# The head of a fused hybrid layer: four column tiles in three chunks, 640 raw columns, rescaling on two engines

## The chip, the cores and the metric

The kernel runs on one core of a Trainium2 chip. A core has five engines that run side by side, each with its own queue of instructions: TensorE (PE in the profile; its weight loads are PEld), VectorE (DVE), ScalarE (ACT), GpSimd (POOL) and SyncE (SP, which here only issues DMAs). An engine works through its queue in order; a semaphore wait at the front of a queue holds all that stands behind it. The metric is the device time of one execution in microseconds; the time before is the median of three runs, 475.52 us (475.46 to 475.56).

## The reference

One decoder layer over 1024 prompt tokens and 64 sample tokens (8 sequences of 8), 1088 token columns in all, in float32:

- `h = rmsnorm(x) * g_norm`, then one projection `proj = h @ w_in` with 3200 output columns, cut into nine parts `Bg, Cg, v, zA, a, g, zB, q, zX`.
- Group A: `Bg * dwconv3(Cg * v) * silu(zA)`. Group B: `u = a * sigmoid(g)`, a causal convolution with 31 taps, a LayerNorm and a swish, times `silu(zB)`. Group X: attention of `q` into 256 memory tokens, whose keys and values come from `rmsnorm(mem)`, times `silu(zX)`.
- The three groups side by side, times `w_out`, plus `x`, and a last RMSNorm. The convolution states and the keys and values are outputs too.

What matters here is that the RMSNorm of a token is one factor, `1/sqrt(mean(x*x)+eps)`, and that a factor per token (a column in the kernel's layout) can be multiplied in before the projection or behind it.

## The kernel before, in words

**Layout.** Channels lie on the partitions and tokens on the columns. The 1024 input channels are 8 slices of 128 (`k` from 0 to 7). The 3200 projected columns are 25 column tiles of 128 (`order`, L260; the first four are a0, a1, a2 and g0, `NHEAD = 4`). A column tile's result for a range of tokens (a chunk) is a sum over the 8 slices in one PSUM bank.

**Precision.** Each float32 value is split into a rounded high part and a low part (`hh`, `hl` for the tokens, `wh`, `wl` for the weights), and a product is three passes: high with high, high tokens with low weights, low tokens with high weights (`pass_k`, L535). So a column tile takes 3 x 8 products per chunk. High parts are made by a cast or copy (for the first four tiles `hw_hi`, L283; on ACT, on GpSimd for the first), low parts by a subtraction on DVE (`hw_lo`, L289).

**Tokens into slices.** x arrives as 9 row tiles of 128 tokens (`xt`, the last with 64). PE transposes a row tile's slice into a PSUM bank (`x_tr`, L235; `sd` banks, four of them), ACT writes `hh` from it times `g_norm` (`x_ev_hi`, L247) and DVE writes `hl` (`x_ev_lo`, L251). Then the bank is free.

**Chunks.** The four head tiles go through the tokens in the chunks of `HEAD` (L33), 256, 256, 256 and 320 columns, all four tiles before the next chunk; the other 21 tiles (`REST`) in chunks of 384, 384 and 320. The `groups` (L166) are the row tiles of each head chunk; `Norm` (L177) takes a group's squares on ACT (`square`, L184), a root on ACT and a short chain on DVE.

**Raw columns.** For the first `RAW = 512` columns the head does not wait for the norm: `hh` and `hl` hold x without its token factor, and the results get the factor when they leave PSUM (`take`, L403), as a row of factors that is the same on all partitions (`rrow`). The row is made by writing a diagonal matrix per row tile (`r_bc`, L1027), transposing it on PE (`r_tr`) and copying it on ACT (`r_cp`, L1042). The other head chunks have their row tiles scaled first (`scale`, `scale_act`). Since the 21 later tiles need scaled slices, the raw columns are later scaled in place, for each k (`rescale`, L218): DVE adds `hh` and `hl` into `t`, multiplies by `rrow`, ACT copies the high part to `hh`, DVE subtracts for `hl`.

**Startup and order.** `startup()` (L995) loads row tiles 0 and 1 in halves (one over ACT's queue), the weights of the head by slice (`hw_load`) and then the rest of x over SP; it runs `WARM` products of the identity on PE ahead of the data. It stands under `tc.manual_schedule()`, so its instructions keep the written order on each engine. The order around the first two chunks is written out, product by product: all four tiles advance together, slice by slice (`p(k, j)`, L1055), with the weight casts, the evacuations, the squares and the factor row between them. Behind it the planner orders the instructions by priority (their order in the program) and by when it reckons them ready; small pieces of work wait in `steps`, one of which `side()` (L119) runs after every fourth product of a pass. There lie the transposes of the fourth chunk, the rescaling, the split of tile 4's weights, the norm of the memory tokens and the transposes of the parameters. The taps of the long convolution are queued on DVE at a lower priority (`run_taps`). SBUF tiles come from one pool of 45 (`big`).

Of the kernel before, what the change touches and what calls it, by code (L numbers as in the profile page):

```python
# [9 lines left out]
F32 = mybir.dt.float32  # L10
# [5 lines left out]
D = 1024  # L16
KT = 8
# [10 lines left out]
L0, L1, L2 = 1, 3, 2  # L28
T1, T2 = 2, 2
TAPPRI = 100  # L30
WARM = 9

HEAD = [(0, 256), (256, 256), (512, 256), (768, 320)]  # L33
REST = [(0, 384), (384, 384), (768, 320)]


NHEAD = 4
RAW = 512


@with_exitstack
def hybrid_trunk_kernel(
# [36 lines left out]
    def B(s, dt=F32, cols=NT):  # L79
        return big.tile([128, cols], dt, tag="b", name=nm(s))  # L80
# [20 lines left out]
    def tr(out, in_, n):  # L101
        T.transpose(out, in_, ident[:n, :n])  # L102
# [60 lines left out]
    xt = [None] * 9  # L163
    xrows = [128] * 8 + [64]
    xcols = [i * 128 for i in range(9)]
    groups = [[0, 1], [2, 3], [4, 5], [6, 7, 8]]  # L166

    def x_src(i):
        return x_prompt[0, i * 128:(i + 1) * 128, :] if i < 8 else x_sample.rearrange("b t d -> (b t) d")

    def x_load(i):
        xt[i] = xt[i] or B("x", cols=D)
        if xrows[i] < 128:
            G.memset(xt[i][xrows[i]:], 0.0)
        nc.sync.dma_start(xt[i][:xrows[i]], x_src(i))

    class Norm:  # L177
        def __init__(self, ts, rows):
# [34 lines left out]
    def x_half(i, h, q):
        if h == 0:
            xt[i] = B("x", cols=D)
        q.dma_start(xt[i][:, h * 512:h * 512 + 512], x_src(i)[:, h * 512:h * 512 + 512])

    def rescale(k):  # L218
        a, b = hh[k][:, :RAW], hl[k][:, :RAW]
        t = B("t", cols=RAW)  # L220
        V.tensor_tensor(t, a.bitcast(F32), b.bitcast(F32), ALU.add)
        V.tensor_tensor(t, t, rrow[0][:, RAW:], ALU.mult)
        S.copy(a, t)
        V.tensor_sub(b, t, a.bitcast(F32))
        dv(1900)

    def gm_T():
        ps = SD()
# [173 lines left out]

    def take(dst, ps, off, n):  # L403
        if rawc[0]:
            V.tensor_tensor(dst, ps[:, :n], rrow[0][:, RAW + off:RAW + off + n], ALU.mult)
            dv(n / 0.96 + 70)
        else:
            S.copy(dst, ps[:, :n])
# [126 lines left out]
    def pass_k(n, c, ps, p, k):  # L535
        off, N = chunks(n)[c]
        h = hl if p == 2 else hh
        mm(
            ps[:, :N], w_block(n, k, p == 1), h[k][:, off:off + N],
            p == 0 and k == 0, p == 2 and k == KT - 1, N / 2.4,  # L540
        )

    def pass_(n, c, ps, p):
# [451 lines left out]
    def startup():  # L995
        V.memset(epst, EPS)
        make_identity(nc, ident)
        x_half(0, 0, nc.sync)
        x_half(1, 0, nc.scalar)
        hw_load(0)  # L1000
        nc.scalar.dma_start(graw, g_norm[0].rearrange("(k p) -> k p", p=128))  # L1001
        hw_load(1, nc.scalar)
        S.activation(warm, epst, AF.Sqrt)
        hw_load(2)
        for i in (0, 1):
            x_half(i, 1, nc.sync)
        for k in (3, 4, 5):
            hw_load(k)
        x_load(2)
        for k in (6, 7):  # L1010
            hw_load(k)
        for i in range(3, 8):
            x_load(i)
        for k in range(KT):
            hh[k] = B("hh", F32R)
            hl[k] = B("hl", F32R)
        wps = MM()
        for _ in range(WARM):
            T.matmul(wps[:, :128], ident, ident, start=True, stop=True)
# [3 lines left out]
        n0, n1, n2, n3 = (Norm([xt[i] for i in g], [xrows[i] for i in g]) for g in groups)  # L1023

        rrow[0] = B("rrow", cols=2 * RAW)

        def r_bc(norm, off):  # L1027
            norm.chain()
            norm.factor()
            for i in (0, 1):  # L1030
                o = off + i * 128
                V.tensor_scalar(rrow[0][:, o:o + 128], ident, 0.0, norm.f[:, i:i + 1], ALU.mult, ALU.add)
            dv(500)

        def r_tr(off):
            ps = SD()
            for i in (0, 1):
                o = off + i * 128
                tr(ps[:, i * 128:i * 128 + 128], rrow[0][:, o:o + 128], 128)
            return ps  # L1040

        def r_cp(off, ps):  # L1042
            S.copy(rrow[0][:, RAW + off:RAW + off + 256], ps[:, :256])

        banks = [SD() for _ in range(4)]
# [13 lines left out]
        def hi(k):
            x_ev_hi(0, k, banks[k])  # L1060

        def lo(k):
            x_ev_lo(0, k, banks[k])

        hw_hi(0, G.tensor_copy)
        hi(0)
        hi(1)
        hw_hi(1, S.copy)
        lo(0)
        lo(1)  # L1070
        hw_lo(0)
        p(0, 0)
        hi(2)
        hi(3)
        hw_hi(2, S.copy)
        hw_lo(1)
        lo(2)
        p(1, 0)
        lo(3)
        p(0, 1)  # L1080
        p(0, 2)
        hw_lo(2)
        p(2, 0)
        x_load(8)
        mem_load()
        load_params()
        nc.sync.dma_start(graw, g_mem[0].rearrange("(k p) -> k p", p=128))
        w_load(NHEAD)
        n0.square(0)
        hw_hi(3, S.copy)  # L1090
        banks += [SD() for _ in range(4)]
        for i in (0, 1):
            for k in range(4, 8):
                x0_tr(k, i)
        p(1, 1)
        p(1, 2)
        for k in range(4, 8):
            hi(k)
        hw_lo(3)
        for k in range(4, 8):  # L1100
            lo(k)
        t1 = []
        for k in range(3, KT):
            if k > 3:
                hw_hi(k, S.copy)
                hw_lo(k)
            p(k, 0)
            p(k - 1, 1)
            p(k - 1, 2)
# [208 lines left out]
```

## Time and profile before

| | |
|---|---|
| median of three runs | 475.52 us |
| profiled execution | 475.39 us |
| its span in the trace | 473.4 us |
| PE busy | 463.8 us (98%) |
| DVE busy | 332.7 us (70%) |
| ACT busy | 228.4 us (48%) |
| GpSimd busy | 4.8 us (1%) |
| first product of the head | 7.14 us |
| first product of column tile 4 | 68.10 us |
| granted TensorE clock | 0.996 |

Times inside the trace count from the start of the span. A row of the timeline gives start, duration, engine, line, operation, the tile written and the tiles read, the shape and how many such instructions stand in a row; in square brackets is how long the engine had been idle and what ended that. DVE's operations all carry L59 and PE's products L95, the lines of the helpers that record them; the tile names tell them apart: `mm` is a projection's result, `sd` a bank for transposes, `junk` a square, `rrow` the factor row. A row of busy times by stretch gives the stretch, its length, then the busy time of PE, PEld, DVE, ACT and POOL with the number of instructions, the granted clock, the DMA share and the GB/s.

### The profile page before, as it was taken

The page shows a single profiled execution, that of the slowest core. Times are in us where ns is not written, and L with a number is a line of the kernel's source. Part 1 is how long each engine was busy: PE and PEld are TensorE (multiplying, and loading weights), DVE is VectorE, ACT ScalarE, POOL GpSimd, SP SyncE. Part 2 cuts the span into 40 slices and gives each one's busy share as a digit, 9 for nine tenths or more (in the row PEclk, how much of TensorE's full clock was granted, in tenths as well). Part 3 has the DMA queues.
Part 4 walks back from the last instruction along what each step waited for, and adds up shares of the span by engine and source line. Part 5 has one row for each costly group of instructions (what it writes and reads, how often), then busy time and mean ns, then how long its engine had stood idle before and what let it go on. Part 6 is the DMA issues. An engine that isn't in the chain of part 4 may idle for free.

```text
span 473.4 us, 7529 instructions
## 1 busy us (share of the span) xinstructions
PE 463.8 (98%) x2933; PEld 435.2 (92%) x2933; DVE 332.7 (70%) x592; ACT 228.4 (48%) x596; POOL 4.8 (1%) x21
## 2 busy tenths in 40 slices
PE   8999999999999999999999999999999999999994
PEld 7998999999999999999999999899999988888884
DVE  3758999999978999997479598833563537333334
ACT  5584668700223649457646455557863534211111
POOL 3000000000000000000000000000000000000000
PEclk9999999999999999999999999999999999999998
DMA  8920163100380400111020531022501553311111
GB/s 296 369 88 3 48 196 109 48 1 0 91 222 9 126 1 2 44 46 46 0 82 10 177 91 45 1 60 90 168 11 44 169 209 117 129 46 44 44 65 70
DMA packets 36447, 40.44 MB, mean 85 GB/s; under 512 B 1743, under 2 KB 30325, under 8 KB 36405
## 3 DMA queue, kind: packets, MB, share of 16 engines
q1 hardware_dynamic: 36109, 39.44, 26.2%
q8 instruction: 23, 0.38, 0.3%
q10 hardware_dynamic: 304, 0.53, 0.3%
q14 instruction: 11, 0.09, 0.1%
HBM read 34.81 MB, written 5.42 MB: 85 GB/s over the span
## 4 chain that ended last, share of the span: by engine, by line
PE 93%; ACT 3%; DMA 1%; DVE 1%; issue 0%; ACTq 0%; DVEq 0%
PE mm L95 81%; PE sd L95 7%; PE sd L102 5%; DMA wr<-in_w_in_dram 1%; ACT sd L881 1%; ACT junk L187 1%; PE sd L866 1%; ACT L146 0%; ACT wh L310 0%; DVE t L59 0%; ACT mh L512 0%; ACT sz L510 0%; ACT wh L287 0%; ACT lnx L868 0%; ACTq L1001 0%
## 5 line engine op out<-in xcount | busy, mean ns | idle before, releaser
L95 PE MATMUL mm<-hh,wh 128*128 128x384 f32 (+2 forms) x632 | 120.1, 325 | 1.4 <-ACT hh L249 1.1
L95 PE MATMUL mm<-hl,wh 128*128 128x384 f32 (+2 forms) x632 | 118.3, 323 | 0.0
L95 PE MATMUL mm<-hh,wl 128*128 128x384 f32 (+2 forms) x632 | 116.5, 322 | 0.0
L59 DVE SCALAR_TENSOR_TENSOR accB<-u,prm,accB 128x1024 f32<-128x1024 f32 x90 | 115.2, 1280 | 1.3
L95 PEld LDWEIGHTS mm<-hh,wh 128*128 128x128 f32 x632 | 102.1, 188 | 4.6 <-ACT hh L249 1.7
L95 PEld LDWEIGHTS mm<-hl,wh 128*128 128x128 f32 x632 | 101.5, 189 | 1.5 <-issue 1.3
L95 PEld LDWEIGHTS mm<-hh,wl 128*128 128x128 f32 x632 | 101.6, 188 | 0.7 <-issue 0.3
L95 PE MATMUL mm<-wol,mh 128*128 128x512 f32 (+1 forms) x136 | 51.2, 377 | 0.0
L95 PE MATMUL mm<-woh,ml 128*128 128x512 f32 (+1 forms) x136 | 51.2, 377 | 0.0
L95 PE MATMUL mm<-woh,mh 128*128 128x512 f32 (+1 forms) x136 | 51.2, 377 | 0.0
L59 DVE TENSOR_TENSOR xres<-mm,xres 128x512 f32<-128x512 f32 (+2 forms) x19 | 12.4, 662 | 37.9 <-PE mm L95 37.7
L944 ACT ACTIVATE sd<-xres 128x512 f32<-128x512 f32 (+1 forms) x16 | 9.6, 600 | 56.1 <-DVE xres L59 56.1
L59 DVE TENSOR_TENSOR wl<-wr,wh 128x512 fp32r<-128x512 f32 x50 | 33.3, 685 | 3.1 <-ACT wh L310 2.5
L95 PEld LDWEIGHTS mm<-woh,ml 128*128 128x128 f32 x136 | 25.6, 188 | 4.7
L95 PEld LDWEIGHTS mm<-woh,mh 128*128 128x128 f32 x136 | 25.6, 188 | 4.7
L95 PEld LDWEIGHTS mm<-wol,mh 128*128 128x128 f32 x136 | 25.6, 188 | 4.7
L712 ACT ACTIVATE P<-sd,nb 128x256 f32<-128x256 f32 x32 | 14.7, 472 | 22.9 <-DVE nb L59 17.9
L362 ACT ACTIVATE prod<-us,prm 128x64 f32<-128x64 f32 x93 | 24.8, 345 | 0.1
L310 ACT CAST wh<-wr 128x512 fp32r<-128x512 f32 x42 | 24.7, 625 | 0.0
L510 ACT ACTIVATE sz<-mm 128x384 f32<-128x384 f32 (+1 forms) x24 | 11.3, 471 | 20.4 <-PE mm L95 20.3
L433 ACT ACTIVATE sig<-mm 128x384 f32<-128x384 f32 (+1 forms) x6 | 2.8, 473 | 37.4 <-PE mm L95 37.3
L249 ACT ACTIVATE hh<-sd,gT 128x256 fp32r<-128x256 f32 (+1 forms) x32 | 14.0, 490 | 8.8 <-PE sd L102 8.7
(195 smaller groups left out, 530.1 us busy)
## 6 DMA issues: line engine op xcount, KB each, us to landing
wr<-in_w_in_dram SPq DMA_DIRECT2D x21, 512.0 KB
wor<-in_w_out_dram SPq DMA_DIRECT2D x8, 512.0 KB
xres<-in_x_prompt_dram SPq DMA_DIRECT2D x8, 512.0 KB
out_dram<-xres SPq DMA_DIRECT2D x7, 512.0 KB
x<-in_x_prompt_dram SPq DMA_DIRECT2D x6, 512.0 KB
cache<-in_cache_mem_k_dram SPq DMA_DIRECT2D x8, 256.0 KB
cache<-in_cache_mem_v_dram SPq DMA_DIRECT2D x8, 256.0 KB
wr<-in_w_in_dram SPq DMA_DIRECT2D x7, 256.0 KB
```

The source lines that it names most:

```text
L59: r = f(*a, **k)
L95: T.matmul(out, lhsT, rhs, start=start, stop=stop)
L102: T.transpose(out, in_, ident[:n, :n])
L187: S.activation(junk[:r], self.ts[i][:r], AF.Square, accum_out=self.ss[:r, i:i + 1])
L249: S.activation(hh[k][:, off:off + n], ps[:, :n], AF.Copy, scale=gT[:, k:k + 1])
L310: S.copy(dst_hi[:, a:b], src[:, a:b])
L362: S.activation(p3[:, k, :], src, AF.Copy, scale=w[:, k0 + k:k0 + k + 1])
L510: S.activation(sz[0][:, off:off + n], ps[:, :n], AF.Silu)
L712: S.activation(P_[i][:, h * 256:h * 256 + 256], bank[h // 2][:, (h % 2) * 256:(h % 2) * 256 + 256], AF.Exp, bias=nb[:, h:h + 1], scale=SCA ...
L866: T.transpose(ps[:, j * 128:j * 128 + 128], accB[j][:, lncols[i]:lncols[i] + 128], ident)
L881: S.activation(junk[:, :384], t, AF.Square, bias=lst["nmu"][:, i:i + 1], accum_out=lst["sq"][:, i:i + 1])
L944: S.activation(junk[:rows], xr[:rows, cs], AF.Square, accum_out=ss[:rows, f:f + 1])
```

## The change

The head goes through three chunks of 256, 384 and 448 columns instead of four. The raw columns are the first two chunks, 640 instead of 512, and the norm groups are row tiles 0 and 1; 2 to 4; 5 to 8. Row tiles 0 and 1 are loaded whole, tile 1 over ACT's queue; the weights of slice 1 move from ACT's queue to SP's, and the order of the loads on SP is new. There is one warm-up product less. The first chunk is one loop over the slices, and in each slice the order of passes is high-high, low tokens, low weights. The sum of `hh` and `hl` in the rescaling moves to GpSimd (`rescale_sum`), with a tile of its own per slice, queued one slice ahead of the rest, which stays on DVE and ACT. The factor row gets its transposes and its copy in one function, behind slice 6 for the first chunk.

```diff
-WARM = 9
-HEAD = [(0, 256), (256, 256), (512, 256), (768, 320)]
+WARM = 8
+HEAD = [(0, 256), (256, 384), (640, 448)]
-RAW = 512
+RAW = 640
...
-    groups = [[0, 1], [2, 3], [4, 5], [6, 7, 8]]
+    groups = [[0, 1], [2, 3, 4], [5, 6, 7, 8]]
...
+    rs = {}
+
+    def rescale_sum(k):
+        rs[k] = B("t", cols=RAW)
+        G.tensor_tensor(rs[k], hh[k][:, :RAW].bitcast(F32), hl[k][:, :RAW].bitcast(F32), ALU.add)
 
     def rescale(k):
-        a, b = hh[k][:, :RAW], hl[k][:, :RAW]
-        t = B("t", cols=RAW)
-        V.tensor_tensor(t, a.bitcast(F32), b.bitcast(F32), ALU.add)
-        V.tensor_tensor(t, t, rrow[0][:, RAW:], ALU.mult)
+        a, b, t = hh[k][:, :RAW], hl[k][:, :RAW], rs[k]
+        V.tensor_tensor(t, t, rrow[0], ALU.mult)
         S.copy(a, t)
         V.tensor_sub(b, t, a.bitcast(F32))
...
     def startup():
...
-        x_half(0, 0, nc.sync)
-        x_half(1, 0, nc.scalar)
+        x_load(0)
+        x_load(1, nc.scalar)
         hw_load(0)
         nc.scalar.dma_start(graw, g_norm[0].rearrange("(k p) -> k p", p=128))
-        hw_load(1, nc.scalar)
         S.activation(warm, epst, AF.Sqrt)
-        hw_load(2)
-        for i in (0, 1):
-            x_half(i, 1, nc.sync)
-        for k in (3, 4, 5):
+        for k in range(1, 5):
             hw_load(k)
         x_load(2)
-        for k in (6, 7):
+        for k in (5, 6):
             hw_load(k)
-        for i in range(3, 8):
+        x_load(3)
+        hw_load(7)
+        for i in range(4, 8):
             x_load(i)
...
+        def r_tr(c):
+            off, n = HEAD[c]
             ps = SD()
+            for o in range(0, n, 128):
+                tr(ps[:, o:o + 128], fb[:, off + o:off + o + 128], 128)
+            S.copy(rrow[0][:, off:off + n], ps[:, :n])
...
+        for k in range(KT):
+            if k == 0:
+                hw_hi(0, G.tensor_copy)
+                hi(0)
+                hi(1)
+            else:
+                hw_hi(k, S.copy)
+            if k < 4:
+                if k > 1:
+                    hi(k)
+                lo(k)
+            hw_lo(k)
             for n in range(NHEAD):
-                pass_k(n, 0, acc[n], j, k)
...
+                pass_k(n, 0, acc[n], 0, k)
+            if k < KT - 1:
+                for j in (2, 1):
+                    for n in range(NHEAD):
+                        pass_k(n, 0, acc[n], j, k)
+            if k in (1, 2):
+                for m in (2 * k + 2, 2 * k + 3):
+                    t0.append(SD())
+                    x0_tr(m, 0)
+                    x0_tr(m, 1)
+            if k in (2, 3):
+                for m in (2 * k, 2 * k + 1):
+                    hi(m)
+                    lo(m)
+            if k == 1:
+                x_load(8)
+                mem_load()
+                load_params()
+                nc.sync.dma_start(graw, g_mem[0].rearrange("(k p) -> k p", p=128))
+                w_load(NHEAD)
+            if k in (3, 4):
+                n0.square(k - 3)
             if k == 5:
-                n0.square(1)
                 r_bc(n0, 0)
             if k == 6:
-                rps = r_tr(0)
+                r_tr(0)
+                n1.square(0)
                 t1 += [x_tr(1, 0), x_tr(1, 1)]
-        r_cp(0, rps)
-        x_ev_hi(1, 0, t1[0])
-        x_ev_hi(1, 1, t1[1])
+        n1.square(1)
+        for k in (0, 1):
+            x_ev_hi(1, k, t1[k])
         for n in range(NHEAD):
-            for j in (1, 2):
-                pass_k(n, 0, acc[n], j, KT - 1)
+            for j in (2, 1):
+                pass_k(n, 0, acc[n], j, KT - 1, 1)
             evac(n, 0, acc[n])
...
-        n1.square(0)
-        n1.square(1)
-        r_bc(n1, 256)
-        n2.square(0)
-        n2.square(1)
+        n1.square(2)
+        r_bc(n1, HEAD[1][0])
+        for i in range(4):
+            n2.square(i)
         n2.chain()
         n2.factor()
         n2.scale_act(0)
         n2.scale(1)
+        n2.scale(3)
+        n2.scale_act(2)
         for n in range(NHEAD):
             pass_(n, 1, acc[n], 1)
-        rps = r_tr(256)
-        r_cp(256, rps)
-        steps.extend([None, None])
+        r_tr(1)
         for k in range(KT):
             steps.append(mk(x_T, 2, k))
-        for i in range(3):
-            n3.square(i)
         for n in range(NHEAD):
             pass_(n, 1, acc[n], 2)
             evac(n, 1, acc[n])
         flush_steps()
-        n3.chain()
-        n3.scale(0)
-        n3.scale(1)
-        n3.scale(2)
...
             startup()
+        w_load(NHEAD + 1)
+        rescale_sum(0)
+        steps.append(mk(params_T, 0))
         for k in range(KT):
-            steps.append(mk(x_T, 3, k))
-        for k in range(KT):
-            steps += [mk(rescale, k), None]
-        for n in range(NHEAD):
-            proj(n, 2)
-        w_load(NHEAD + 1)
+            steps += [mk(rescale_sum, k + 1) if k < 7 else None, mk(rescale, k)]
         for h in range(2):
             steps.append(mk(w_split, NHEAD, h))
         steps.append(mem_norm)
-        for j in range(3):
-            steps += [mk(params_T, j), None]
+        for j in (1, 2):
+            steps.append(mk(params_T, j))
         steps.append(gm_T)
         for n in (0, 3, 1, 2):
-            proj(n, 3)
+            proj(n, 2)
         flush_steps()
```

More of the change, by code (lines that the diff above doesn't have):

```diff
@@ L165, in hybrid_trunk_kernel, with x_load @@
     xcols = [i * 128 for i in range(9)]
-    groups = [[0, 1], [2, 3], [4, 5], [6, 7, 8]]
+    groups = [[0, 1], [2, 3, 4], [5, 6, 7, 8]]
     def x_src(i):
         return x_prompt[0, i * 128:(i + 1) * 128, :] if i < 8 else x_sample.rearrange("b t d -> (b t) d")
-    def x_load(i):
+    def x_load(i, q=nc.sync):
         xt[i] = xt[i] or B("x", cols=D)
@@ L174, in x_load @@
             G.memset(xt[i][xrows[i]:], 0.0)
-        nc.sync.dma_start(xt[i][:xrows[i]], x_src(i))
+        q.dma_start(xt[i][:xrows[i]], x_src(i))
     class Norm:
@@ L211, in scale @@
                 dv(660)
[L213 to L216, printed above, removed]
+    rs = {}
+    def rescale_sum(k):
+        rs[k] = B("t", cols=RAW)
+        G.tensor_tensor(rs[k], hh[k][:, :RAW].bitcast(F32), hl[k][:, :RAW].bitcast(F32), ALU.add)
     def rescale(k):
-        a, b = hh[k][:, :RAW], hl[k][:, :RAW]
-        t = B("t", cols=RAW)
-        V.tensor_tensor(t, a.bitcast(F32), b.bitcast(F32), ALU.add)
-        V.tensor_tensor(t, t, rrow[0][:, RAW:], ALU.mult)
+        a, b, t = hh[k][:, :RAW], hl[k][:, :RAW], rs[k]
+        V.tensor_tensor(t, t, rrow[0], ALU.mult)
         S.copy(a, t)
         V.tensor_sub(b, t, a.bitcast(F32))
-        dv(1900)
+        dv(1500)
     def gm_T():
@@ L404, in take @@
         if rawc[0]:
-            V.tensor_tensor(dst, ps[:, :n], rrow[0][:, RAW + off:RAW + off + n], ALU.mult)
+            V.tensor_tensor(dst, ps[:, :n], rrow[0][:, off:off + n], ALU.mult)
             dv(n / 0.96 + 70)
@@ L533, in evac, with pass_k @@
             {"g": ev_g, "a": ev_a, "q": ev_q, "cg": ev_cg, "v": ev_v, "bg": ev_bg}[kind](c, ps, j)
-    def pass_k(n, c, ps, p, k):
+    def pass_k(n, c, ps, p, k, last=2):
         off, N = chunks(n)[c]
@@ L539, in pass_k @@
             ps[:, :N], w_block(n, k, p == 1), h[k][:, off:off + N],
-            p == 0 and k == 0, p == 2 and k == KT - 1, N / 2.4,
+            p == 0 and k == 0, p == last and k == KT - 1, N / 2.4,
         )
@@ L1022, in startup @@
         xt[8] = B("x", cols=D)
-        n0, n1, n2, n3 = (Norm([xt[i] for i in g], [xrows[i] for i in g]) for g in groups)
-        rrow[0] = B("rrow", cols=2 * RAW)
+        n0, n1, n2 = (Norm([xt[i] for i in g], [xrows[i] for i in g]) for g in groups)
+        rrow[0] = B("rrow", cols=RAW)
+        fb = B("fb", cols=RAW)
         def r_bc(norm, off):
@@ L1029, in r_bc, with hi, lo @@
             norm.factor()
-            for i in (0, 1):
+            for i in range(norm.n):
                 o = off + i * 128
-                V.tensor_scalar(rrow[0][:, o:o + 128], ident, 0.0, norm.f[:, i:i + 1], ALU.mult, ALU.add)
-            dv(500)
-        def r_tr(off):
+                V.tensor_scalar(fb[:, o:o + 128], ident, 0.0, norm.f[:, i:i + 1], ALU.mult, ALU.add)
+        def r_tr(c):
+            off, n = HEAD[c]
             ps = SD()
[L1037 to L1045, printed above, removed]
-        def x0_tr(k, i):
-            tr(banks[k][:, i * 128:i * 128 + 128], xt[i][:, k * 128:(k + 1) * 128], 128)
+            for o in range(0, n, 128):
+                tr(ps[:, o:o + 128], fb[:, off + o:off + o + 128], 128)
+            S.copy(rrow[0][:, off:off + n], ps[:, :n])
+        t0 = [SD() for _ in range(4)]
+        def x0_tr(k, i):
+            tr(t0[k][:, i * 128:i * 128 + 128], xt[i][:, k * 128:(k + 1) * 128], 128)
+        def hi(k):
+            x_ev_hi(0, k, t0[k])
+        def lo(k):
+            x_ev_lo(0, k, t0[k])
         for i in (0, 1):
@@ L1053, in startup @@
         acc = [MM() for _ in range(NHEAD)]
-        def p(k, j):
-            for n in range(NHEAD):
-                pass_k(n, 0, acc[n], j, k)
[L1059 to L1109, printed above, removed]
+        t1 = []
+        for k in range(KT):
[10 more added lines that the diff above has]
+            hw_lo(k)
+            for n in range(NHEAD):
+                pass_k(n, 0, acc[n], 0, k)
[20 more added lines that the diff above has]
+                n0.square(k - 3)
```

## The prediction

> **What bounds the kernel now.** I read the page first, then the busy time in two stretches, the head (first product to the first product of tile 4, 7.14 to 68.10 us) and the rest.
>
> ```profile
> span 473.4 us, 7529 instructions
> ...
> PE 463.8 (98%) x2933; PEld 435.2 (92%) x2933; DVE 332.7 (70%) x592; ACT 228.4 (48%) x596; POOL 4.8 (1%) x21
> ```
> ```profile
> 7.14:68.10 60.96, 59.59 (x463) 57.63 (x463) 50.22 (x129) 41.40 (x89) 2.70 (x9) 1.00 0.45 154
> 68.10:473.40 405.30, 398.79 (x2446) 372.60 (x2444) 282.13 (x462) 184.89 (x504) 0.20 (x2) 1.00 0.23 72
> ```
>
> PE sets the time, and everything that the change touches lies before 68.10. So the question is when tile 4 starts. The profiled execution took 475.39 us, 1.99 more than its span and 0.13 under the median of the runs; my sum goes against 475.39, and I add the 0.13 at the end.
>
> PE's busy figure hides short waits, so I take its pace from the starts of unbroken rows of its timeline:
>
> ```profile
> 10.23 1.03 PE L102 MATMUL sd<-ident,x 128*128 128x128 f32 x8
> ...
> 26.63 4.01 PE L95 MATMUL mm<-hh,wl 128*128 128x256 f32 x32
> ...
> 348.53 1.58 PE L95 MATMUL mm<-hh,wh 128*128 128x384 f32 x8
> ...
> 356.88 1.33 PE L95 MATMUL mm<-hh,wh 128*128 128x320 f32 x8
> ...
> 360.39 1.58 PE L95 MATMUL mm<-hh,wh 128*128 128x384 f32 x8
> ...
> 419.65 0.39 PE L95 MATMUL mm<-woh,mh 128*128 128x512 f32 x1
> ...
> 425.55 0.39 PE L95 MATMUL mm<-wol,mh 128*128 128x512 f32 x1
> ```
>
> A transpose costs (1.03-0.27)/7 = 0.109, where 0.27 is one transpose's own duration; a product of 256 columns (4.01-0.28)/31 = 0.1203; of 384, 48 in 8.35 us, 0.1740; of 320, 24 in 3.51 us, 0.1463; of 512, 26 in 5.90 us, 0.2269. Columns alone would make these proportional; they are not, each product has some 0.013 us of its own.
>
> The head holds 96 products a chunk (4 tiles, 8 k, 3 passes): 96 x (3 x 0.1203 + 0.1463) = 48.69; 77 transposes behind 7.14, 8.39; the small g_mem one 0.16. That is 57.24 of 60.96: **PE waits 3.72 us in the head.** The largest pieces:
>
> ```profile
> 7.14 0.71 PE L95 MATMUL mm<-hh,wh 128*128 128x256 f32 x4 [0.33 <-ACT hh L249]
> 8.21 0.74 PE L95 MATMUL mm<-hh,wh 128*128 128x256 f32 x4 [0.36 <-ACT wh L287]
> ...
> 34.70 0.71 PE L95 MATMUL mm<-hl,wh 128*128 128x256 f32 x4
> 36.17 1.11 PE L95 MATMUL mm<-hh,wh 128*128 128x256 f32 x3 [0.76 <-ACT hh L249]
> ```
>
> Four products need 0.48, so the second row is 0.6 late (a weight cast) and the fourth 1.0 (ACT was squaring the last row tiles).
>
> **The change part by part.**
>
> *Fewer products.* 448 columns lie midway between 384 and 512: 0.2005. 96 x (0.1203 + 0.1740 + 0.2005) = 47.50, **-1.19** (bounds of the 448 price, 0.1740 to 0.2269, give -3.7 to +1.3; the straight line is taken). One more transpose of a factor, **+0.11**.
>
> *The start.* Row tiles 0 and 1 come whole, so 1.31 MB (x0, x1, first weights) must land before the first product, where 0.79 MB did.
>
> ```profile
> 0.00:6.03 6.03, 4.65 (x22) 4.41 (x23) 0.23 (x2) 1.49 (x2) 0.83 (x10) 1.00 0.64 199
> ```
> ```profile
> 1.38 4.21 PE L1019 MATMUL mm<-ident 128*128 128x128 f32 x18 [1.38 <-POOL ss L182]
> ...
> 5.72 1.09 PE L102 MATMUL sd<-ident,x 128*128 128x128 f32 x8
> ...
> 6.03 0.61 POOL L287 CAST wh<-wr 128x512 fp32r<-128x512 f32 x1 [4.66 <-DMA wr<-in_w_in_dram]
> ...
> 6.52 0.84 ACT L249 ACTIVATE hh<-sd,gT 128x256 fp32r<-128x256 f32 x2 [2.86 <-PE sd L102]
> ...
> 7.03 0.88 DVE L59 SCALAR_TENSOR_TENSOR hl<-sd,gT,hh 128x256 fp32r<-128x256 f32 x2 [1.04 <-ACT hh L249]
> ```
>
> When the first weights were there (6.03, GpSimd's cast) 199 GB/s x 6.03 = 1.20 MB had moved: a third of it already belonged to later loads. In the new order nothing but x0, x1 and those weights is ahead, so 1.31 MB are there 0.11 MB, some 0.3 to 0.4 us, later. x0 and x1 lie on two queues (SP and ACT) and land before the weights; from there the steps are the old ones (cast 0.61, product). First product near 7.5: **+0.36**. Bounds: 0, and the whole 0.52 MB at 199 GB/s, +2.6; the value near 0 is taken because the moved bytes are counted, the other end assumes that no byte of the 1.20 MB was spare. The weights of k=7 now stand behind four row tiles: 4.2 MB, even at 199 GB/s 21 us, and ACT comes to them at 22 (below), so the rest of SP's new order costs nothing; ACT's queue issues one DMA fewer. x8, memory and parameters are issued about as early as before, for work behind 47 us.
>
> *The order on ACT.* Startup is ordered by hand, and the trace shows ACT keeping to it:
>
> ```profile
> 9.30 1.07 ACT L187 ACTIVATE junk<-x 128x1024 f32<-128x1024 f32 x1
> ...
> 10.35 0.61 ACT L287 CAST wh<-wr 128x512 fp32r<-128x512 f32 x1
> ...
> 12.41 1.16 ACT L287 CAST wh<-wr 128x512 fp32r<-128x512 f32 x2
> ...
> 13.45 1.08 ACT L187 ACTIVATE junk<-x 128x1024 f32<-128x1024 f32 x1
> ...
> 14.65 0.30 ACT L146 ACTIVATE y<-ss,epst 128x2 f32<-128x2 f32 x1
> ...
> 16.37 1.29 DVE L59 TENSOR_TENSOR wl<-wr,wh 128x512 fp32r<-128x512 f32 x2
> ...
> 17.82 0.38 PE L102 MATMUL sd<-ident,rrow 128*128 128x128 f32 x2
> ...
> 18.24 0.37 ACT L1043 COPY rrow<-sd 128x256 f32<-128x256 f32 x1 [2.26 <-PE sd L102]
> 18.51 0.84 ACT L249 ACTIVATE hh<-sd,gT 128x256 fp32r<-128x256 f32 x2
> ...
> 21.29 0.84 ACT L249 ACTIVATE hh<-sd,gT 128x256 fp32r<-128x256 f32 x2 [1.94 <-PE sd L102]
> ...
> 25.28 1.05 ACT L187 ACTIVATE junk<-x 128x1024 f32<-128x1024 f32 x1
> ...
> 29.90 0.29 ACT L146 ACTIVATE y<-ss,epst 128x2 f32<-128x2 f32 x1
> ...
> 31.22 1.15 ACT L205 ACTIVATE x<-x,f 128x1024 f32<-128x1024 f32 x1 [1.02 <-DVE f L59]
> 32.27 0.35 ACT L1043 COPY rrow<-sd 128x256 f32<-128x256 f32 x1
> ```
> ```profile
> L59 DVE SCALAR_TENSOR_TENSOR hl<-sd,gT,hh 128x256 fp32r<-128x256 f32 x24 | 10.5, 477 | 3.0 <-ACT hh L249 2.9
> ```
>
> ACT sat idle for 2.26 and 1.94 us, yet row tile 2 was squared only at 25.28: within startup nothing overtakes. From these rows, start to start: a cast holds ACT 0.51 (1.16 less one of 0.65), a square 1.04 (9.30 to 10.35), an hh evacuation 0.37 (0.84 less 0.47), a factor copy 0.27 (18.24 to 18.51), a row-tile scaling 1.05 (31.22 to 32.27). Handovers: last transpose to ACT 0.31 (17.93 to 18.24), cast to its product 0.67 (7.54, where the cast began, to 8.21), hh evacuation to hl 0.51 (6.52 to 7.03), square to root 1.20 (13.45 to 14.65), root to row-tile scaling 1.32 (29.90 to 31.22), root through the factor chain to the next weight subtraction 1.72 (14.65 to 16.37).
>
> In the old order the casts ran ahead of PE. The new order puts evacuations, squares and the factor copy between the casts, some of them behind PE's own work. Per k PE has 12 products, 1.44 us; 4 of them 0.48. PE then waits:
>
> - k=3: the transposes of slice 7 need slice 3's bank, whose evacuation stands behind those of slices 4 and 5 and a cast. Counted from the last transpose of slice 5: 0.09+0.37+0.37+0.51+0.51+0.48 (its hl) = 2.33, less PE's 0.11+1.44+0.22: **0.56**.
> - k=4: evacuation 7, a square, the cast, from the last transpose: 0.31+0.37+1.04+0.67 = 2.39, less 0.11+1.44: **0.84**. k=5: the second square lies between the casts, 0.51+1.04 less 1.44: **0.11**.
> - k=6: the low weights stand behind the factor chain on DVE. From k=5's cast: 0.64+0.60 (its subtraction), 1.59 (1.72, the root being done), 0.73 = 3.56, less 0.67+1.44+0.96: **0.49**.
> - k=7: the factor copy waits for PE's k=6, then a square, then the cast: 0.11+0.31+0.27+1.04+0.67 = 2.40, less 8 transposes (0.87): **1.53**; its low half another **0.10**.
> - chunk 1: a bank late, **0.10**. Then ACT does, behind its last evacuation, a square, a root, four squares, a root, two row-tile scalings: 0.31+0.47+1.20+0.20+4.32+1.32+1.05+1.20 = 10.07 from PE's last transpose to row tile 7; PE has 9.71 (0.11, 16 products 2.78, 32 products 5.57, 0.33, 0.70, 0.22): **0.36**. This takes the place of the 1.0 at 36.17.
>
> Together 4.09 against 3.72: **+0.37**. Ends: -2.7 if ACT is not held behind PE at k=4, 6 and 7 (1.4 left of the 4.09), +2.0 if one more square (1.04) and four slower handovers come in.
>
> *The rescaling.* Per k DVE loses one operation of three; the two left grow to 640 columns.
>
> ```profile
> L59 DVE TENSOR_TENSOR t<-t,rrow 128x512 f32<-128x512 f32 x8 | 5.4, 685 | 0.0
> ...
> L59 DVE TENSOR_TENSOR u<-mm,rrow 128x256 f32<-128x256 f32 x6 | 2.3, 417 | 3.5 <-PE mm L95 2.8 <-ACT rrow L1043 0.8
> ...
> masks.py:199 POOL TENSOR_SCALAR_AFFINE_SELECT ident<-ident 128x128 f32<-128x128 f32 x1 | 0.3, 292 | 0.0
> ```
> ```profile
> 60.97 0.69 DVE L59 TENSOR_TENSOR hl<-t,hh 128x512 fp32r<-128x512 f32 x1
> ```
>
> 512 columns hold DVE 0.60 (two in 1.29); the slope is (685-417)/256 = 1.05 ns a column, so 640 hold it 0.735: 16 x 0.735 = 11.8 against 24 x 0.60 = 14.4. The old rescaling ended at 61.66, 6.4 ahead of tile 4; it was hidden under PE's chunks, so the 2.6 that DVE gains are worth **0**, as are the fewer evacuations and the dropped third group of factors. GpSimd's addition is not in the trace: between its cast's 1.2 ns a column (0.76 for 640) and the select's 2.3 (1.46). I take 1.46, as the select too does more than copy: 8 are 11.7 us, beside 20 us of chunk-2 products, cost 0. If that cover is gone, DVE's products with the factor row are late, and tile 4's first pass behind them. The Trainium skill (GPSIMD Engine Reference, 3.1 Elementwise — side-by-side cycle accounting) gives some 2.6 cycles an element at 1.2 GHz for such an add, an estimate of 1.39; the sum would stay.
>
> Sum: -1.19+0.11+0.36+0.37 = **-0.35**: 475.0 against the profile's 475.39, 475.2 as a median. Tile 4 would begin at 67.75, chunk 1 end near 47.4. 0.2% (0.95 us) is about what a measurement of this kernel can tell from no change.
>
> **The rivals.**
>
> 1. *ACT is not held up* (faster). If the casts run ahead of PE after all, the -2.7 replaces the +0.37: 475.2-3.1 = 472.1; half of it 473.6. For it: ACT is busy 41.4 of 60.96 us, there is room. Against: the 2.26 us idle in front of a ready square.
>
> 2. *GpSimd's sums hold up the rescaling* (slower). If all sums come behind 47.4 and DVE's operations cannot run beside them, each k costs 1.46+1.47: 23.4 us, to 70.8. Tile 4's pass needs the last hh at 67.75+7 x 0.174 = 69.0, 1.8 before it is there; each of the taps that DVE takes in between adds its length, over 1 us. 477 to 480, say 478. It decides from a sum of 1.25 us on (8 x (1.25+1.47) = 21.7, what there is up to 69.0). Against: GpSimd is busy for 2.7 of the head's 60.96 us, and the sums could start once chunk 1's slices are evacuated, long before 47.4. The Trainium skill (SBUF — State Buffer, Who interferes with whom) has this as a rule: a VectorE operation with two SBUF inputs and a GpSimd operation that reads SBUF take one port pair as an exclusive lock. No trace of before shows the two side by side.
>
> 3. *PE is still slow when x arrives.* The 18 warm-up instructions took (4.21-0.42)/17 = 0.22 each, the transposes of the same shape 0.109: PE ran at half pace until some time before 5.9. With 16 of them and then a pause until x lands, it may stay there. Price: half of the time until it wakes, at most the same 4.3 us, so 0 to 2.1; about 1.2, since part of it is waiting anyway: 476.4. The Trainium skill (TensorE: Matmul & The Clock Gate, What's actually happening) says that the clock opens after a busy window of about 3.4 us that runs freely; 16 warm-ups fill 3.5, with nothing to spare.
>
> 4. *The new order costs more*: the +2.0 in place of +0.37, 476.8.
>
> **How the numbers follow.** The forecast with its own spread, 474.2 to 476.1 (starts from 7.1 to 8.2, waits 0.5 either way): 0.47, of which 0.04 is faster by over 0.2% and 0.03 slower. Rival 1: 0.28, all faster. Rival 2: 0.10 and rival 4: 0.05, all slower. Rival 3: 0.10, of which 0.04 within. Faster 0.32, within 0.44, slower 0.24. The range leaves out the far quarter of rival 1 and rival 2: 472.9 to 477.1.
>
> **What would show it.** First product near 7.5, tile 4 near 67.8. PE 1.5 us idle ahead of its k=7 products, ended by ACT's weight cast, and 0.8 ahead of k=4. No wait over 0.5 near 36 to 40. GpSimd's sums at 0.8 to 1.5 us, the last hl subtraction before 66, no wait of PE at tile 4. I am wrong if chunk 0 has no wait over 0.5, if the first product is past 8.5 or its pace is not 0.12, or if PE waits for DVE or GpSimd at tile 4.

## The result, and the profile after

The changed kernel takes 483.22 us (median; 481.60 to 483.41) against 475.54 us for the kernel before on the same chip: **slower by 1.5%**, ratio 1.0151 with a 95% interval of 1.0138 to 1.0164. The prediction said 475.2, with a range that ended at 477.1. The profiled execution is the one of 481.60, the fastest.

The top of the page after:

```profile
span 479.8 us, 7303 instructions
...
PE 464.1 (97%) x2836; PEld 433.0 (90%) x2836; DVE 336.6 (70%) x570; ACT 230.7 (48%) x586; POOL 17.6 (4%) x29
```

PE is busy as long as before (463.8), though it has 97 instructions fewer; GpSimd went from 4.8 to 17.6 us. The same two stretches as in the prediction, the head and the rest:

```profile
7.33:73.40 66.07, 60.14 (x368) 56.09 (x368) 51.99 (x92) 41.75 (x77) 15.72 (x17) 0.97 0.41 138
73.40:479.80 406.40, 398.94 (x2445) 372.39 (x2443) 284.22 (x477) 186.82 (x507) 0.20 (x2) 1.00 0.23 72
```

The head grew from 60.96 to 66.07 us and the rest from 405.30 to 406.40; the granted clock of the head is 0.97 where it was 1.00. PE's waits by what it waited for, with their sum, number and longest:

```profile
PE sd L102 <- ACT x L205: 3.7, 2, 3.1
PE mm L95 <- ACT wh L286: 2.0, 2, 1.4
...
PE sd L102 <- DVE mem L59: 1.2, 1, 1.2
```

The second row is what the prediction expected of ScalarE's order. The first and third are new: the transposes of row tiles 5 to 8 wait for their scaling, and at 79 us those of the memory tokens for theirs. Chunk by chunk, from the first product of each to that of the next, for a kernel of the experiments (e7) whose chunks hold the same work, and the kernel changed:

| | chunk 0 | chunk 1 | chunk 2 | first product of tile 4 |
|---|---|---|---|---|
| after | 7.33, 17.33 long | 24.66, 27.86 long | 52.52, 20.88 long | 73.40 |
| e7 | 7.37, 15.16 long | 22.53, 22.33 long | 44.86, 20.88 long | 65.74 |

So chunk 1 is 5.53 us longer than in e7, and chunk 0 is 2.17 longer. The chain that ended last, in chunk 1 (start, length, and the work that stood on the chain then):

```profile
30.96 0.30 ACT y L146
...
32.29 3.33 DVE fb L59 x3
35.63 1.47 DVE v L59
37.09 0.09 DVE y L59
...
37.21 1.41 DVE t L59
...
38.64 1.47 DVE t L59
...
40.53 2.20 ACT x L205 x2
```

It isn't made of squares or of PE, but of operations on 128 by 128 and 128 by 4 elements: `fb` writes the diagonal of factors, `v` and `t` are steps of the norm of row tiles 5 to 8. The timeline shows what ran beside them, and the groups how long each is on average (busy us, mean ns):

```profile
32.38 7.69 POOL L217 TENSOR_TENSOR t<-hh,hl 128x640 f32<-128x640 f32 x5 [14.86 <-ACT junk L187]
```
```profile
L217 POOL TENSOR_TENSOR t<-hh,hl 128x640 f32<-128x640 f32 x8 | 12.9, 1648 | 27.4 <-ACT junk L187 14.9 <-PE sd L102 12.5
```
```profile
L59 DVE TENSOR_SCALAR v<-ss 128x4 f32<-128x4 f32 x1 | 1.5, 1547 | 0.0
L59 DVE TENSOR_TENSOR t<-y,v 128x4 f32<-128x4 f32 x1 | 1.4, 1395 | 0.0
...
L59 DVE SCALAR_TENSOR_TENSOR hl<-sd,gT,hh 128x448 fp32r<-128x448 f32 x8 | 5.5, 682 | 1.5 <-ACT hh L248 1.3
...
L59 DVE TENSOR_SCALAR v<-ss 128x2 f32<-128x2 f32 x2 | 0.3, 165 | 0.0
```

Five of the sums ran back to back from 32.38 to 40.07. Of the VectorE operations between them, two of the three `fb`, `v` and two `t` steps each took about as long as a sum: `v` on four columns 1.547 us, on two columns elsewhere in the same kernel 0.165. Not all did: the reciprocal at 37.01, which reads one tile, took its 0.16 beside a running sum. The evacuation `hl<-sd,gT,hh`, which reads a PSUM bank and one SBUF tile, kept its 0.68, also at 54.75, where a sum ran beside it.

The pause that follows, 3.1 us of PE, had an effect of its own, seen in the stretches behind it (PE busy, ..., granted clock third from the end):

```profile
40.00:42.00 2.00, 0.27 (x2) 0.20 (x2) 1.86 (x5) 1.47 (x2) 0.07 (x1) 1.00 0.00 0
42.00:44.00 2.00, 1.40 (x7) 1.23 (x6) 0.83 (x1) 1.58 (x3) 0.00 (x0) 0.70 0.04 8
44.00:46.00 2.00, 2.00 (x9) 1.90 (x8) 1.42 (x2) 1.12 (x3) 0.00 (x0) 0.50 0.00 0
46.00:48.00 2.00, 2.00 (x16) 1.93 (x15) 1.70 (x3) 1.51 (x3) 0.00 (x0) 0.95 0.00 0
```

PE is fully busy from 44 to 46, at half clock: nine instructions where the next 2 us have sixteen. The three shortfalls, (0.30+0.50+0.05) x 2, make up to 1.7 us, less what PE was still idle; this is an estimate from the rows.

### The profile page after: what moved, and what is told of

The parts are those of the page before. It is cut to its first block, busy times and chain, and to the rows that moved or that the text cites. A ratio compares the mean times of both kernels' runs of the same rounds, so it can differ in the third digit from the quotient of the medians.

```text
span 479.8 us, 7303 instructions
## 1 busy us (share of the span) xinstructions
PE 464.1 (97%) x2836; PEld 433.0 (90%) x2836; DVE 336.6 (70%) x570; ACT 230.7 (48%) x586; POOL 17.6 (4%) x29
## 4 chain that ended last, share of the span: by engine, by line
PE 84%; DVE 8%; ACT 5%; DMA 1%; issue 1%; ACTq 0%; DVEq 0%
PE mm L95 72%; PE sd L95 6%; PE sd L102 5%; DVE hl L59 2%; DVE t L59 2%; ACT sd L880 1%; DMA graw<-in_g_norm_dram 1%; ACT junk L187 1%; DVE fb L59 1%; DVE accB L59 1%; PE sd L865 1%; DVE wl L59 1%; ACT x L205 0%; ACT hh L248 0%; DVE us L59 0%
## 5 line engine op out<-in xcount | busy, mean ns | idle before, releaser
L95 PE MATMUL mm<-hh,wh 128*128 128x384 f32 (+3 forms) x600 | 117.3, 332 | 2.4 <-ACT wh L286 2.0
L95 PE MATMUL mm<-hl,wh 128*128 128x384 f32 (+3 forms) x600 | 119.0, 333 | 0.0
L95 PE MATMUL mm<-hh,wl 128*128 128x384 f32 (+3 forms) x600 | 115.2, 329 | 0.1
L95 PEld LDWEIGHTS mm<-hh,wh 128*128 128x128 f32 x600 | 99.6, 188 | 5.1 <-ACT wh L286 2.5
L95 PEld LDWEIGHTS mm<-hl,wh 128*128 128x128 f32 x600 | 100.4, 190 | 1.9 <-issue 1.3
L95 PEld LDWEIGHTS mm<-hh,wl 128*128 128x128 f32 x600 | 99.9, 188 | 1.6 <-issue 0.3
L59 DVE TENSOR_TENSOR xres<-mm,xres 128x512 f32<-128x512 f32 (+2 forms) x19 | 12.4, 662 | 38.3 <-PE mm L95 38.1
L248 ACT ACTIVATE hh<-sd,gT 128x256 fp32r<-128x256 f32 (+2 forms) x24 | 13.0, 563 | 11.1 <-PE sd L102 10.9
```

The source lines that it names most:

```text
L59: r = f(*a, **k)
L95: T.matmul(out, lhsT, rhs, start=start, stop=stop)
L248: S.activation(hh[k][:, off:off + n], ps[:, :n], AF.Copy, scale=gT[:, k:k + 1])
```

## The experiments

Theory A: GpSimd's sums hold up VectorE's small operations, and that is most of the loss. Theory B: the norm of four row tiles is late by itself. Kernels e1, e2 and e4 start from the changed kernel, e3 from the one before. Each ratio is against the kernel before on the same chip. The kernel before takes 475.47 us on the chip of e1 to e4, 475.75 on that of e5 to e8 and 475.30 on that of e9 and e10, so a difference of two medians from different chips can be off by up to 0.5 us.

**e1, the sums back on VectorE.**

```diff
-        G.tensor_tensor(rs[k], hh[k][:, :RAW].bitcast(F32), hl[k][:, :RAW].bitcast(F32), ALU.add)
+        V.tensor_tensor(rs[k], hh[k][:, :RAW].bitcast(F32), hl[k][:, :RAW].bitcast(F32), ALU.add)
```

> Edit: the changed kernel with the eight sums of hh and hl back on VectorE; nothing else. Theory A (GpSimd's sums block VectorE's small operations of the norm chain between 32 and 40 us, each of which grew to the length of a sum): fb, v and the two products of the chain take 0.2 to 0.3 us again, PE's waits between 38 and 43 fall from 4.0 to at most 0.6, the first product of tile 4 comes at 68.5 to 70.0 instead of 73.4, and the time is 477 to 479 (483.2 less 4 to 6). VectorE gets 8 x 0.73 = 5.9 us more to do, which should lie under PE. Theory B (the norm of four row tiles is late by itself: more squares, a longer queue on ScalarE): PE still waits 3 us or more near 38, time 482.5 to 484.

Measured: 477.37 us, ratio 1.003 (1.002 to 1.004). One engine's name is worth 5.85 us; theory B is out as the main cause. The wait is not gone, though. Counted from when the next PE instruction would have started, the two waits for the row tiles' scaling were 3.3 and 0.8 us, 4.0 together; two of 0.7 are left, 1.5 together, since two of VectorE's own sums now sit between the steps of the norm:

```profile
36.70 0.17 DVE L59 TENSOR_SCALAR v<-ss 128x4 f32<-128x4 f32 x1 [1.01 <-ACT junk L187]
...
37.13 0.79 DVE L59 TENSOR_TENSOR t<-hh,hl 128x640 f32<-128x640 f32 x1
37.84 0.16 DVE L59 TENSOR_TENSOR t<-y,v 128x4 f32<-128x4 f32 x1
37.91 0.82 DVE L59 TENSOR_TENSOR t<-hh,hl 128x640 f32<-128x640 f32 x1
38.65 0.16 DVE L59 TENSOR_TENSOR t<-t,y 128x4 f32<-128x4 f32 x1
...
40.45 0.44 PE L102 MATMUL sd<-ident,x 128*128 128x128 f32 x2 [0.56 <-ACT x L205]
...
41.48 0.44 PE L102 MATMUL sd<-ident,x 128*128 128x128 f32 x2 [0.60 <-ACT x L205]
```

**e2, the sums on GpSimd, but behind the norm chain.**

```diff
         rs[k] = B("t", cols=RAW)
+        G.tensor_copy(rs[k][:, 0:1], rrow[0][:, RAW - 1:RAW])
         G.tensor_tensor(rs[k], ...)
```

> Edit: the changed kernel; ahead of each sum GpSimd copies one column of the last factor row into the sum's tile, so that no sum starts before chunk 1's factor row is there (near 42). Theory A: the norm chain is as fast as with the sums on VectorE, PE's waits between 38 and 43 at most 0.6; the sums now meet VectorE's rescaling in the last chunk, where each sum of 1.6 us holds up one subtraction (2.0 instead of 0.8). Eight times 1.2 = 9.6 us of VectorE's time lie in a chunk of 20 us: tile 4 at 69 to 72, time 477 to 481. Theory B: PE waits 3 us or more near 38, 482.5 to 484.

Measured: 480.69 us (478.48 to 481.57), ratio 1.0104 (1.0076 to 1.0132). The waits of the row tiles went (0.34 near 38, counted as for e1), but PE waited 0.8 us at 46.46 for one of VectorE's `hl` evacuations. Tile 4 began at 68.89, 4.5 earlier, and yet little of it was kept: the held-up rescaling pushed the norm of the memory tokens behind tile 4's start, and PE paused for it and then ran at half clock.

```profile
75.83 0.64 PE L102 MATMUL sd<-ident,mem 128*128 128x128 f32 x2 [2.41 <-DVE mem L59]
```
```profile
75.00:77.00 2.00, 1.17 (x5) 1.17 (x6) 2.00 (x4) 0.00 (x0) 0.00 (x0) 0.73 0.00 0
77.00:79.00 2.00, 2.00 (x11) 1.90 (x10) 1.08 (x2) 0.72 (x2) 0.00 (x0) 0.50 0.00 0
```

**e3, the kernel before with only the sums on GpSimd.** In `rescale`, `V.tensor_tensor(t, a.bitcast(F32), b.bitcast(F32), ALU.add)` becomes `G.tensor_tensor(...)` with the same operands.

> Edit: the kernel before, with nothing changed but the sum of hh and hl (512 columns) moved from VectorE to GpSimd. Theory A: sums of 512 x 2.45 ns = 1.25 us start as soon as the slices of the first two chunks are complete (near 27) and stretch the small operations of the chains behind them (roots at 29.90 and later) to 1.2 us each; 2 to 4 us of waits of PE between 30 and 48, time 477.5 to 479.5. Theory B: the sums hurt nobody, 475.0 to 476.0.

Measured: 478.27 us, ratio 1.0059 (1.0044 to 1.0074), and the same picture at 512 columns:

```profile
28.87 1.53 DVE L59 TENSOR_SCALAR rrow<-ident,f 128x128 f32<-128x128 f32 x2
28.97 2.59 POOL L221 TENSOR_TENSOR t<-hh,hl 128x512 f32<-128x512 f32 x2 [17.04 <-ACT junk L187]
30.32 1.26 DVE L59 TENSOR_SCALAR v<-ss 128x2 f32<-128x2 f32 x1
...
33.68 0.44 PE L102 MATMUL sd<-ident,x 128*128 128x128 f32 x2 [1.35 <-ACT x L205]
...
47.67 0.52 PE L102 MATMUL sd<-ident,x 128*128 128x128 f32 x3 [1.34 <-DVE x L59]
```

The harm belongs to the engine of the sum and not to the new chunks. Pauses of 1.35 us left the clock at 1.00.

**e4, the weight casts of k = 4 to 7 earlier on ScalarE.**

```diff
-            else:
+            elif k < 4:
                 hw_hi(k, S.copy)
...
+            if 3 <= k < KT - 2:
+                for m in ((4, 5) if k == 3 else (k + 2,) if k + 2 < KT else ()):
+                    hw_hi(m, S.copy)
             if k in (2, 3):
```

> Edit: the changed kernel with the casts of the weights of k = 4 to 7 issued on ScalarE one or two slices earlier, ahead of the evacuations, squares and the factor copy behind which they stood. The waits that the prediction put at k = 4 (0.84) and k = 7 (1.53), measured at 0.84 and 1.5, should go: PE's waits in chunk 0 behind k = 3 from 2.7 to at most 0.5. By itself that is 2.2 us. Theory A says that the sums on GpSimd start when the slices are complete and the norm chain is on the same engines, so both move forward together and most of it is kept: 481.0 to 482.0. If the chain near 38 is set by ScalarE's row of squares instead, which begins with the end of chunk 0's work on ScalarE, PE loses it again there: 483 and a wait near 38 of 5 to 6 us.

Measured: 480.97 us, ratio 1.0118 (1.0103 to 1.0133). The waits of 0.84 and 1.52 went, but not the sum of them: the next thing in line was the subtraction for k = 6 behind the factor chain on VectorE.

```profile
19.83 0.48 DVE L59 TENSOR_SCALAR fb<-ident,f 128x128 f32<-128x128 f32 x2
20.23 1.28 DVE L59 TENSOR_TENSOR wl<-wr,wh 128x512 fp32r<-128x512 f32 x2
20.97 0.74 PE L95 MATMUL mm<-hh,wl 128*128 128x256 f32 x4 [1.13 <-DVE wl L59]
```

The expectation had not looked at VectorE's queue. Its median is 2.25 better than the changed kernel's; the profile shows chunk 0 shorter by only 0.45 us, in an execution whose first products ran slowly (next), so how the 2.25 divides stays open.

**e5, e1 with ten warm-up products.** In e1 the runs lay at 476.1 to 476.2 and at 477.4 to 477.7. Its profile is of the upper group:

```profile
5.92 1.97 PE L102 MATMUL sd<-ident,x 128*128 128x128 f32 x8
...
7.91 1.19 PE L95 MATMUL mm<-hh,wh 128*128 128x256 f32 x4
```

Eight transposes take 1.97 us where before has 1.09, four products 1.19 instead of 0.71: PE at half pace, as in its warm-up (the granted-clock column reads 1.00 here, so the pace is the evidence). In the profile of the changed kernel, the execution of 481.60, the same rows read 1.09 and 0.71. The edit is `WARM = 10` for `WARM = 8`.

> Edit: the kernel with the sums on VectorE (e1), and ten warm-up products instead of eight (20 instructions of 0.21 us, 1.4 to 5.6). In e1's profile the first eight transposes take 1.97 us instead of 1.09 and the first eleven products 0.21 instead of 0.12, the chain's start is 7.9 instead of 7.3, and its runs lie in two groups, 476.1 to 476.2 and 477.4 to 477.7. Theory C (the pause of 0.56 us between the warm-up and the data leaves PE slow in some executions, rival 3 of the prediction): with the pause filled all runs are in the lower group, 476.0 to 476.4, transposes at 0.11. Rival: the two groups come from the landing of the loads, which the warm-up does not move: both groups stay, median 477.2 to 477.5.

Measured: 476.31 us (476.22 to 476.99), ratio 1.0018 (1.0009 to 1.0027), 1.06 below e1; no run is left at 477.4 or above. By the means it is 0.5, since four of e1's ten runs were in the lower group already. Without the sums on GpSimd the new chunks and the new order are thus no gain and hardly a loss.

**e9, the changed kernel with ten warm-up products.**

> Edit: the changed kernel with ten warm-up products instead of eight, the sums left on GpSimd. Its own times lie at 481.6 (once) and 483.2 to 483.4 (three times). Theory C (PE still slow at the first products in the executions of the upper group): all runs near 481.6, against a median of 483.2, and what is left over the kernel before is 6 us. Rival (the groups come from something else, such as the landing of the loads): median stays near 483.2.

Measured: 481.97 us (481.32 to 482.17), ratio 1.0137 (1.0122 to 1.0153), 1.25 below the changed kernel. Two of its four runs, at 482.17, lie between the changed kernel's 481.6 and its 483.2 to 483.4. In this profile the pause is gone, and still PE's first three transposes took 0.21 to 0.27 each, the rest 0.11. The pause is therefore not shown to be what makes PE slow. The profiles of e2 and e8, with eight warm-up products and pauses of 0.91 and 1.00 us, have the eight transposes in 1.09: there PE came to full pace within the warm-up, near 4.2 and 4.3 us. In e1 it came to it near 9.7. What the runs show is that this moment differs from one execution to the next, and that a longer warm-up lowered both medians.

**e6, e5 with the weights ahead on both engines.** The casts as in e4, and `hw_lo(6)` ahead of the factor chain at k = 5.

> Edit: e5, and in chunk 0 the casts of the weights of k = 4 to 7 one or two slices earlier on ScalarE, the subtraction for k = 6 ahead of the factor chain on VectorE. The waits of 0.84 (k = 4), 0.29 (k = 6) and 1.52 (k = 7) should go, 2.6 us together, against e5's 476.2. If all of it is kept: 473.6, faster than the kernel before by 1.9. If the row of squares and the chain of the four row tiles set the next chunk's start, PE gives back what it gains there (waits near 38 of 3 to 4 us instead of 1.5): 475.5 to 476.2.

Measured: 473.89 us, ratio 0.9963 (0.9951 to 0.9976). Nearly all is kept, 2.42 of 2.6: **faster than the kernel before**.

**e7, e6 with VectorE's sums behind the norm chain.** The one-column copy of e2, on VectorE.

> Edit: e6, and each VectorE sum preceded by a copy of one column of the last factor row, so that no sum runs between the operations of the norm chain (in e1 two sums of 0.8 us sat in it, between 37.1 and 38.7). Against e6 PE's waits near 38 to 41 should fall by 1.0 to 1.5 us, if they are set by that chain: 472.5 to 473 where e6 is 473.6, or 474.3 to 475 where e6 is near 475.8. If the waits come from ScalarE's row-tile scalings alone (1.05 us each, two in a row), nothing changes against e6.

Measured: 472.86 us, ratio 0.9947 (0.9934 to 0.9959), 1.03 below e6, the fastest version found. From the root of the last group to its first scaling it takes 33.11 to 34.45, 1.34 us; in the changed kernel it was 35.45 to 40.53, 5.08.

```profile
33.11 0.30 ACT L146 ACTIVATE y<-ss,epst 128x4 f32<-128x4 f32 x1
...
34.45 2.19 ACT L205 ACTIVATE x<-x,f 128x1024 f32<-128x1024 f32 x2 [1.04 <-DVE f L59]
```

**e10, e7 with the sums on GpSimd**, in the same place.

> Edit: the kernel of e7 with the sums on GpSimd, each behind a one-column copy of the last factor row on GpSimd, so that they run behind the norm chain. Theory A: PE's waits near 36 to 41 are as small as in e7 (0.4), but the sums of 1.6 us hold up VectorE's subtractions and products of the last chunk; as in e2 the last subtraction comes 1 us behind tile 4's start and the memory's norm is late, with waits of 2 to 4 us at 70 to 77: 475 to 477.5, against 472.9 with the sums on VectorE. If the split is worth what it takes off VectorE (8 x 0.73 us), with the sums out of the norm chain: 472 to 473.

Measured: 477.78 us, ratio 1.005 (1.0033 to 1.0067): 4.9 us worse than e7, with nothing changed but the engine of the sums and of their one-column copies, and a little more than expected. The groups of VectorE tell what the split is worth, first e10, then e7:

```profile
L59 DVE TENSOR_TENSOR t<-t,rrow 128x640 f32<-128x640 f32 x8 | 9.3, 1192 | 0.8 <-POOL t L218 0.8
L59 DVE TENSOR_TENSOR hl<-t,hh 128x640 fp32r<-128x640 f32 x8 | 7.3, 937 | 0.1
```
```profile
L59 DVE TENSOR_TENSOR t<-hh,hl 128x640 f32<-128x640 f32 x8 | 6.6, 820 | 0.0
L59 DVE TENSOR_TENSOR hl<-t,hh 128x640 fp32r<-128x640 f32 x8 | 6.5, 824 | 0.1
L59 DVE TENSOR_TENSOR t<-t,rrow 128x640 f32<-128x640 f32 x8 | 6.4, 817 | 0.0
```

VectorE is rid of 6.6 us of sums and pays 2.9 + 0.8 = 3.7 of it back in longer operations, while each sum takes 1.55 to 2.15 us where VectorE needs 0.82. PE's pause for the memory tokens (2.4 us) and the half clock behind it are back, as in e2.

**e8, GpSimd copies hh in place of adding.** `G.tensor_copy(rs[k], hh[k][:, :RAW].bitcast(F32))` stands for the sum; the low part is left out of the rescaled columns.

> Edit: the changed kernel with GpSimd copying hh into the sum's tile in place of adding hh and hl (the low part is left out of the rescaled columns). It tells whether a GpSimd operation must read two SBUF inputs to hold up VectorE's small operations. Theory A1 (any GpSimd operation that reads SBUF): fb, v, t of the chain stretch to the length of the copy, 0.8 to 1.6 us each. Theory A2 (only one with two inputs): they take 0.16 to 0.28 as they do alone. By the time: A1 near 478 to 482, depending on the copy's length, A2 near 477.

Measured: 475.04 us, one execution, below what either theory expected. The place where a copy met the chain looks like this:

```profile
32.38 1.14 DVE L59 TENSOR_SCALAR fb<-ident,f 128x128 f32<-128x128 f32 x3
32.45 0.80 POOL L217 COPY t<-hh 128x640 f32<-128x640 f32 x1 [14.84 <-ACT junk L187]
```

The three `fb` take 0.68 in e1 and 1.14 here, 0.46 more: one of them waited out the copy, which reads one SBUF tile. So a second input is not needed; only a few operations met a copy, though, and not each of the chain, as A1 had it. That the time is nevertheless so much better than 483 fits the copies being half as long and not back to back but 1.04 us apart, as ScalarE's squares are: `v`, at 35.54, started just ahead of one and took 0.17, and of the steps behind it only one was stretched, from 0.16 to 0.22.

## Why the prediction was wrong

*Fewer products, one more transpose.* Held. Eight 448-column products take 1.62 us, 0.2026 each (0.2005 taken).

*The start.* First product at 7.33 in the profile (7.5 forecast), with PE at full pace. In other executions it is not: see rival 3.

*The order on ScalarE.* Held in its two large places: 0.84 ahead of k = 4, 1.52 ahead of k = 7, both ended by the weight cast. The bank wait of 0.56 at k = 3 did not come, as four transposes ran in a row there; the one at k = 6 was 0.29 and not 0.49. By chunk 0's length the whole was close: 17.33 less 11.55 of products and 2.40 of its 22 transposes is 3.4, against 3.6 forecast; e6 and e7 take 2.2 of it back. What failed is the *row tile 7: 0.36*. It was worked out with 1.32 us from the root to the scaling. That figure is right for a chain that has VectorE to itself (1.34 in e7), but the sums come between its operations. On VectorE they cost 1.2 us (chunk 1 is 23.52 long in e6, 22.33 in e7), and on GpSimd 4.1 more (27.86 in the kernel changed, 23.75 in e5), the half clock included.

*The rescaling: 0.* This is the step that failed. Its price was about right (1.46 taken, 1.54 to 1.63 measured and once 2.16; the upper bound was too low), its place was not. The sums were laid "beside 20 us of chunk-2 products"; five of eight ran from 32.38 on, in the stretch where VectorE's small operations set PE's next transposes. Their slices were complete and GpSimd had nothing else to do; the profile names a square on ScalarE as what let the first one start. Perhaps the sum took the SBUF tile that the square freed; no run tests this. Nor does 0 hold once the sums are kept behind the norm chain: in e10 they run from 38.3 to 54.4, the later ones beside chunk 2's products, and cost 4.9 us against e7. Its signs fell with it: a wait of 3.1 us near 40 where none over 0.5 was to be, and the last `hl` subtraction at 73.29 instead of before 66. The signs that it named for being wrong looked at chunk 0, the first product and tile 4, and none at chunk 1, where most of the time went.

*Rival 2* had the mechanism and gave it 0.10, at the wrong place. It counted the sums behind 47.4, held each against VectorE's 1.47 us of rescaling for the same slice, and named it as evidence *against* that they "could start once chunk 1's slices are evacuated, long before 47.4". That early start was the harm: an operation of 0.16 us that meets a sum of 1.55 takes about nine times its own length. Where the sums ran behind the chain (e2, e10), they held up the rescaling as this rival says, but PE paid at the memory tokens' transposes and with the half clock, not in tile 4's first pass. The Trainium skill (SBUF — State Buffer, Who interferes with whom) says that whoever issues first gets the shared port pair for the whole instruction and the other fully blocks; the trace agrees, `v` and the `t` steps taking 1.4 to 1.55 us beside sums of 1.55.

*Rival 3*, PE slow at the first products, is true of part of the executions, and priced right: 1.2 us forecast, 1.25 between the changed kernel and e9, 1.06 between e1 and e5. The pause that it names as the reason is not shown (see e9). It was made an alternative to the others, though it adds to them. *Rival 1* is out by the waits of 0.84 and 1.52; its price has a slip, since 1.4 us left, against 3.72, are -2.3 and not -2.7. *Rival 4*, the order costing more, is right in direction: without GpSimd's sums (e5) the head waits 5.6 us, against 4.09 forecast and 5.72 (3.72 + 2.0) in that rival.

*Missing from the list*: that a long pause of PE is paid twice, and that a late rescaling drags what stands behind it. In the profile after, the memory's norm came behind the sigmoid and the first taps, and PE waited 1.2 us for it; e1, e5 and e7 don't have that wait.

The ledger, by medians, from 475.2 to 483.2: the sums on GpSimd 5.85 (483.22 to 477.37), the longer warm-up 1.06 (477.37 to 476.31), and 1.1 that e5 still lies above the forecast. In e5's profile tile 4 starts 1.72 later than forecast. By the forecast's own terms chunk 1 is 22.28 long (96 products of 0.1740, 47 transposes, 0.46 of waits) and chunk 2 20.39; in e5 they are 23.75 and 20.88, while chunk 0 is 0.26 shorter than forecast. Of the 1.47 in chunk 1, 1.1 is the row tiles' scaling (two waits of 0.7 against 0.36); the rest is the price of a 448-column product and small gaps.

## What to carry to other kernels

An idle engine doesn't make an operation free. Before moving work to GpSimd, see when it *can* start, not when it is wanted, and list the short VectorE operations that it may meet on the way to PE: each can wait for a whole GpSimd instruction. When it can start depends on more than its inputs: here the profile named a square on another engine. Where work is moved off an engine, compare with the same work left there but put behind the critical chain; here that, with weights prepared ahead and a longer warm-up, turned +1.5% into -0.5%.

## What the runs showed of the hardware

- A GpSimd operation that reads SBUF held VectorE operations of both kinds, the products of two SBUF tiles (`t`, 1.40 and 1.45 us instead of 0.16) and the scalings of one (`v`, 1.55 instead of 0.17), until it ended; those that read PSUM and one SBUF tile kept theirs (0.68), and so did a reciprocal of one SBUF tile (0.16). It goes the other way too: a sum that started behind a VectorE subtraction (54.11 in the profile after) took 2.16 us instead of 1.57.
- The clock fell to 0.50 behind pauses of PE of 3.1 us (after) and 2.41 us (e2), once the work had resumed, and was full again some 3.4 us after it fell (42.8 to 46.2 in the profile after); it did not fall behind the pauses of 1.35 us in e3. The Trainium skill (TensorE: Matmul & The Clock Gate, What's actually happening) has the drop behind an idle window of about 3.4 us; the 2.41 us here were enough, and the measurement decides.
- The same section of the Trainium skill lets the clock open after about 3.4 us of work. Warm-ups of 3.8 us (e1) and 4.6 us (e9) still left slow transposes at 6 us in some executions; in e2 PE came to full pace near 4.2 us, in e1 near 9.7.
